# Split weights interleaved, every second GEMM group run backward, other places for rows and weights, and no widened products, in a two-layer decoder trunk

## The chip, the core and the metric

The kernel runs on one core of a Trainium2 chip. The time is the device time of one execution in microseconds. Two runs of the kernel before took 2280.04 and 2280.48 us, median 2280.26 us. The profile comes from one execution with the hardware profiler on.

The engines are named as in the profile: PE is TensorE (matrix products), PEld its loads of stationary operands, DVE is VectorE, ACT is ScalarE, POOL is GpSimd, SP is SyncE, which here only issues DMAs.

## The reference

The input is 256 rows of 2048 features with 16 meta tokens in front (272 rows in all), and two layers follow. Layer 0 is a forgetting attention, layer 1 a stick-breaking attention whose keys and values come from one shared projection. Each layer ends in a squared-ReLU MLP of width 8192. Cut to its matrix products:

```python
a = rms_norm(h, norm_attn[0]); q, k, v, f = split(a @ fox_w_in[0])     # 2048 -> 3*2048 + 16
h = h + forgetting_attention(q, k, v, cumsum(log_sigmoid(f + b))) @ fox_w_o[0]
h = h + square(relu(rms_norm(h, norm_mlp[0]) @ w_up[0])) @ w_down[0]   # 2048 -> 8192 -> 2048
a = rms_norm(h, norm_attn[1]); k, v = split(rms_norm(h, kv_norm) @ w_kv)
h = h + stick_breaking_attention(a @ sb_w_q[0], k, v) @ sb_w_o[0]
h = h + square(relu(rms_norm(h, norm_mlp[1]) @ w_up[1])) @ w_down[1]
return rms_norm(h, final_norm)[16:]
```

Everything is float32. After the keys and values of layer 1, the 16 meta rows are needed no more.

## The kernel before

**Split operands.** Activations are kept with features on the 128 partitions, as 16 chunks of 128 features by T = 272 rows. A GEMM is made from split operands: each float32 is written as a high part (a copy to `fp32r`) and a low part (the difference), and a product is three products: high by high, low rows by high weights, high rows by low weights.

**Groups.** All GEMMs go through `gemm_group`. One group takes 2048 input features and 512 output features. It holds four PSUM accumulators (`accs[m]`, 128 output features each) and loops over four blocks `kb` of 512 input features, each of four chunks `kc`. That makes 4 x 4 x 4 x 3 = 192 products; the stationary operand of each is a 128x128 piece of split weights, and the moving operand is one chunk of split rows: 272 columns in layer 0 and in the shared keys and values (t0 = 0), 256 columns where the meta rows are left out (t0 = 16, `M`). The variable `u` counts the groups from 1 to 96. The last one, u = 96, is `token_group`: there the rows are stationary and the 512 weight columns move.

The order of stages is: 12 groups for queries, keys and values of layer 0 with the attention among them; 4 for its output projection; 32 for its MLP (for each of four quarters `f` of the width 4 up and 4 down); 4 for the queries of layer 1; 8 for the shared keys and values; 4 for the output projection; 31 plus the token group for the MLP of layer 1.

**Weights.** `weights` loads one block of weights for one `kb` with two DMAs on SP's queue into two tiles `raw` (2 chunks by 512 columns each), four buffers deep, and splits them: ACT copies to the high part (L225), DVE subtracts for the low part (L226). The high and the low parts are in tiles of their own (`whi`, `wlo`, [128, 2, 576], four buffers each), and 512 of the 576 columns are used from `o1` on: 0 at t0 = 0, 16 at t0 = 16.

**Rows.** `Split` holds split rows: 16 chunks with a stride of XROW = 640 elements, the high part at element `hi` of a chunk's stretch, the low part at `lo`. `ROWS` gives these places: (48, 368) at t0 = 0 and (0, 320) at t0 = 16.

**Widened products.** At t0 = 16, `Split` fills six columns behind the 256 of the high rows with zeros (on POOL, L135). In every group with u % 4 == 1 there, and in the group u = 90, three products on the high rows run over 262 columns rather than 256 (`wide`). What they add behind column 256 of the accumulator is not read.

**Order on the engines.** A scheduler places the instructions. Products are kept in the order of the program; other matrix products (attention scores, transposes, norms) come between them. The evacuation of an accumulator belongs to the end of its group: `evac` reads `accs[m][:, :n]` on DVE, and the output of the up stage is squared and split again into the rows `u` (`Split(f"u{layer}_{f}", t0)`).

Of the kernel before, what the change touches and what calls it, by code (L numbers as in the profile page):

```python
# [10 lines left out]
F32R = mybir.dt.float32r  # L11
# [4 lines left out]
P = 128  # L16
D = 2048
NC = D // P
# [6 lines left out]
N_FF = 4  # L25

ROWS = {0: (48, 368), M: (0, 320)}
XROW = 640

G_A0, G_M0, G_KV, G_A1, G_M1, G_FIN = range(6)  # L30
# [3 lines left out]
def yoco_kernel(ctx: ExitStack, tc: tile.TileContext, hT_in, gains, b_f, w_f, w_qkv0, w_o0, w_up, w_dn,  # L34
                w_kv, w_q1, w_o1, g_row, out):
    nc = tc.nc
# [5 lines left out]
    wspl = ctx.enter_context(tc.tile_pool(name="wspl", bufs=4))  # L42
# [72 lines left out]
    pad = align.tile([P, 32], F32, name="pad")  # L115
# [5 lines left out]
    class Split:  # L121


        def __init__(self, label, t0):
            n = T - t0
            self.t0 = t0
            rows = xs.tile([P, NC * XROW + 64], F32R, tag="x", name=f"x_{label}")
            hi, lo = ROWS[t0]
            rows = rows[:, hi:hi + NC * XROW].rearrange("p (c t) -> p c t", c=NC)
            d = lo - hi  # L130
            self.hi, self.lo = rows[:, :, :n], rows[:, :, d:d + n]
            if t0:

                self.wide = rows[:, :, :n + 6]
                nc.gpsimd.tensor_copy(rows[:, :, n:n + 6], pad[:, :6].unsqueeze(1).to_broadcast([P, NC, 6]))  # L135

    def split_chunk(sp, gi, c):

# [47 lines left out]
    def behind(ins, other):  # L186
        tc.add_manual_dep(ins.ins, other.name, mybir.DependencyInfo(mybir.DependencyClass.NoSync,
                                                                    mybir.DependencyReason.DATA))

    def gemm_matmul(*args, **kw):  # L190

        ins = nc.tensor.matmul(*args, **kw).ins  # L192
# [8 lines left out]
    def weights(u, kb, wblk, o1, load_x=None):  # L201

        src_w = wblk[kb].rearrange("p (k c) -> p k c", k=4)
        piece = 1 if load_x is not None and kb < 2 else 2
        raws = [wraw.tile([P, 2, 512], F32, tag="raw", name=f"raw_{u}_{kb}_{hf}") for hf in range(2)]
        for k0 in range(0, 4, piece):
            if load_x is not None:
                load_x(range(4 * kb + k0, 4 * kb + k0 + piece))
            if load_x is not None and kb == k0 == 0:

                for c0 in (0, 256):
                    nc.scalar.dma_start(raws[0][:, 0, c0:c0 + 256], src_w[:, 0, c0:c0 + 256])
            else:
                nc.sync.dma_start(raws[k0 // 2][:, k0 % 2:k0 % 2 + piece], src_w[:, k0:k0 + piece])
        parts = []
        for hf in range(2):
            whi, wlo = (wspl.tile([P, 2, 576], F32R, tag=f"w{x}", name=f"w{x}_{u}_{kb}_{hf}") for x in ("hi", "lo"))
            whi, wlo = whi[:, :, o1:o1 + 512], wlo[:, :, o1:o1 + 512]
            boxes = [(o, piece, 0, 512) for o in range(0, 2, piece)]
            if load_x is not None and kb == hf == 0:  # L220
                boxes[:1] = [(0, 1, 0, 256), (0, 1, 256, 512)]
            for o, no, c0, c1 in boxes:
                src = raws[hf][:, o:o + no, c0:c1]
                hp, lp = whi[:, o:o + no, c0:c1], wlo[:, o:o + no, c0:c1]
                on_act = nc.scalar.activation(hp, src, AF.Copy)  # L225
                on_dve = nc.vector.tensor_tensor(out=lp, in0=src, in1=hp.bitcast(F32), op=ALU.subtract)  # L226
            parts.append((whi, wlo))
        return parts, on_act, on_dve

    def gemm_group(wblk, sp, t0, evac, before={}, after={}, load_x=None):  # L230

        uid[0] += 1
        u = uid[0]
        accs = [pacc.tile([P, 512], F32, tag="acc", name=f"acc_{u}_{m}") for m in range(4)]
        n = T - t0
        for kb in range(4):
            if kb in before:
                before[kb]()  # L240
            parts, on_act, on_dve = weights(u, kb, wblk, 16 if t0 else 0, load_x)
            if kb in after:
                with tc.issue_after(on_act.ins), tc.issue_after(on_dve.ins):
                    after[kb]()

            if load_x is not None and kb == 0:
                runs = [([kc], range(4)) for kc in range(4)]
            elif kb in (0, 3):
                runs = [(range(4), [m]) for m in range(4)]
            else:  # L250
                runs = [(range(2 * hf, 2 * hf + 2), range(4)) for hf in range(2)]
            pinned[0] = load_x is None
            for kcs, ms in runs:
                pairs = ((0, sp.hi), (0, sp.lo), (1, sp.hi))
                if t0:
                    products = [(kc, m, *pair) for pair in pairs for kc in kcs for m in ms]
                else:
                    products = [(kc, m, *pair) for m in ms for kc in kcs for pair in pairs]
                left = {m: 3 * len(kcs) for m in ms}

                wide = [(0, 0, 0), (1, 0, 1), (2, 1, 1)] if t0 and u % 4 == 1 else []
                if u == 90:

                    wide = [(0, 0, 0), (0, 0, 1), (0, 2, 1)]
                for kc, m, part, x in products:
                    first, left[m] = kb == kc == 0 and left[m] == 3 * len(kcs), left[m] - 1
                    nw = n
                    if m == (0 if u == 90 else 3) and x is sp.hi and (kb, kc, part) in wide:
                        x, nw = sp.wide, n + 6
                    gemm_matmul(accs[m][:, :nw], parts[kc // 2][part][:, kc % 2, m * P:(m + 1) * P], x[:, 4 * kb + kc],  # L270
                                start=first, stop=kb == kc == 3 and left[m] == 0)
                if kb == 3:
                    for m in ms:
                        evac(m, accs[m][:, :n])

    def token_group(wblk, sp, done):


        uid[0] += 1
        u = uid[0]  # L280
# [12 lines left out]

        for kb in range(2):
            parts.append(weights(u, kb, wblk, 16)[0])
            for b in range(2):
                products(b, [kb])
        for kb in (2, 3):
            parts.append(weights(u, kb, wblk, 16)[0])
# [324 lines left out]
    def mlp(layer, xm, norm, t0, last_evac, last_group=None):  # L624
# [5 lines left out]
        for f in range(N_FF):  # L630
            u = Split(f"u{layer}_{f}", t0)
            for g in range(4):
                def evac(m, acc, g=g):
                    c = 4 * g + m
                    r = tmp.tile([P, T], F32, tag="relu", name=f"relu_{layer}_{f}_{c}")
                    u2 = tmp.tile([P, T], F32, tag="u2", name=f"u2_{layer}_{f}_{c}")
                    nc.vector.scalar_tensor_tensor(out=r[:, t0:], in0=acc, scalar=0.0, in1=box["r"][:, t0:],
                                                   op0=ALU.max, op1=ALU.mult)
                    nc.scalar.activation(u2[:, t0:], r[:, t0:], AF.Square)
                    nc.scalar.activation(u.hi[:, c], u2[:, t0:], AF.Copy)  # L640
                    nc.vector.tensor_tensor(out=u.lo[:, c], in0=u2[:, t0:], in1=u.hi[:, c].bitcast(F32),
                                            op=ALU.subtract)
                gemm_group(w_up[layer, f, g], xm, t0, evac, {2: get_rstd} if f == g == 0 else {})
                if last_group is not None and f == N_FF - 1 and g == 0:
                    to_token_major()
            for g in range(4):
# [304 lines left out]
```

## Time and profile before

| what | value |
|---|---|
| median time, two runs | 2280.26 us |
| span of the profiled execution | 2278.5 us |
| time around the span, against the median | 1.8 us |
| HBM read, written | 413.85 MB, 8.41 MB |
| mean DMA rate | 187 GB/s |
| DVE busy | 1333.5 us |
| ACT busy | 1065.1 us |

The span is the time from the first to the last instruction of the profiled execution. A row of a group of instructions gives line, engine, operation, output and inputs by the program's names, shapes and count, then busy time and the mean duration of one, then the idle time of the engine ahead of it and what ended it. The mean duration of a product is from its issue to its modelled end; products overlap, so the next one starts well before that. The view of the chain of waits in order of time gives the start, the length and what ran; "x192" behind it is the number of instructions in the run, so length by number is the distance from one start to the next.

The weights come in by these issues (line 6 of the page: destination and source, queue, count, size, time to landing), and none of them stands in the chain outside the first microseconds:

```profile
raw<-w_up SPq DMA_DIRECT2D x256, 512.0 KB, 3.9
raw<-w_dn SPq DMA_DIRECT2D x256, 512.0 KB, 4.0
```

### The profile page before, as it was taken

The numbers are of one execution on the slowest core, as the hardware profiler recorded it, in microseconds if no ns is written. First come the engines' busy times: TensorE is split into PE (matmuls) and PEld (weight loads), VectorE is DVE, ScalarE is ACT, GpSimd is POOL, SyncE is SP. The second block draws the span as 40 slices with busy tenths as digits, with TensorE's granted clock in tenths as the row PEclk, the third lists the DMA queues.
The fourth block names the chain that finished last, engine by engine and source line by source line (L and its number), as shares of the span: only waits on it lengthen the run. The fifth ranks groups of instructions, "written<-read, shape, count | busy, mean of one in ns | idle before, by whom it ended". The sixth has DMA issues, their size and how long they took to land.

```text
span 2278.5 us, 44956 instructions
## 1 busy us (share of the span) xinstructions
PE 2271.1 (100%) x18898; PEld 2262.8 (99%) x18898; DVE 1333.5 (59%) x1930; ACT 1065.1 (47%) x1471; POOL 39.4 (2%) x72
## 2 busy tenths in 40 slices
PE   9999999999999999999999999999999999999998
PEld 9999999999999999999999999999999999999998
DVE  7767566554455455455566666666555555555555
ACT  6444445443354344335445555555443544543554
POOL 1000000000000000000000000000000000000001
PEclk9999999999999999999999999999999999999999
DMA  7765665555555555555556555555656556566564
GB/s 238 228 198 188 222 184 176 181 172 180 182 176 185 167 185 179 174 185 169 186 183 193 168 174 169 167 185 190 202 187 201 192 189 201 184 200 195 186 201 141
DMA packets 146171, 425.19 MB, mean 187 GB/s; under 512 B 31648, under 2 KB 43824, under 8 KB 145968
## 3 DMA queue, kind: packets, MB, share of 16 engines
q1 hardware_dynamic: 113760, 406.29, 54.1%
q10 hardware_dynamic: 32208, 16.02, 2.6%
q8 instruction: 148, 2.42, 0.4%
q14 instruction: 55, 0.45, 0.1%
HBM read 413.85 MB, written 8.41 MB: 185 GB/s over the span
## 4 chain that ended last, share of the span: by engine, by line
PE 99%; DMA 0%; issue 0%; POOL 0%; SPq 0%; POOLq 0%; ACT 0%; DVE 0%
PE acc L192 97%; PE po L435 0%; PE ps L435 0%; PE pza L435 0%; DMA raw<-w_qkv 0%; PE pzb L735 0%; PE po L804 0%; PE ps L508 0%; PE po L603 0%; PE pf L354 0%; PE pta L757 0%; PE pta L756 0%; PE pv L394 0%; POOL ob L850 0%; PE ptb L709 0%
## 5 line engine op out<-in xcount | busy, mean ns | idle before, releaser
L226 DVE TENSOR_TENSOR wlo<-raw,whi 128x1024 fp32r<-128x1024 f32 (+1 forms) x773 | 928.5, 1216 | 715.6 <-ACT whi L225 706.6
L225 ACT ACTIVATE whi<-raw 128x1024 fp32r<-128x1024 f32 (+1 forms) x773 | 796.4, 1050 | 961.0 <-PE acc L192 913.4
L192 PE MATMUL acc<-x_m,whi 128*128 128x272 f32 (+1 forms) x4096 | 643.1, 282 | 0.0
L192 PE MATMUL acc<-x_u,whi 128*128 128x272 f32 (+1 forms) x3968 | 626.0, 282 | 0.0
L192 PEld LDWEIGHTS acc<-x_m,whi 128*128 128x128 f32 x4096 | 566.0, 188 | 0.1
L192 PEld LDWEIGHTS acc<-x_u,whi 128*128 128x128 f32 x3968 | 550.4, 188 | 0.0
L192 PE MATMUL acc<-x_m,wlo 128*128 128x272 f32 (+1 forms) x2048 | 441.4, 282 | 0.0
L192 PE MATMUL acc<-x_u,wlo 128*128 128x272 f32 (+1 forms) x1984 | 432.1, 282 | 0.0
L192 PE MATMUL acc<-x_a,whi 128*128 128x272 f32 (+1 forms) x2048 | 355.4, 286 | 0.2 <-ACT whi L225 0.2
L192 PEld LDWEIGHTS acc<-x_m,wlo 128*128 128x128 f32 x2048 | 323.5, 188 | 0.0
L192 PEld LDWEIGHTS acc<-x_u,wlo 128*128 128x128 f32 x1984 | 315.3, 188 | 0.0
L192 PEld LDWEIGHTS acc<-x_a,whi 128*128 128x128 f32 x2048 | 301.3, 189 | 1.7 <-ACT whi L225 1.1
L192 PE MATMUL acc<-x_a,wlo 128*128 128x272 f32 (+1 forms) x1024 | 253.8, 286 | 0.0
L192 PE MATMUL acc<-x_kv,whi 128*128 128x272 f32 x1024 | 191.7, 288 | 0.0
L192 PEld LDWEIGHTS acc<-x_a,wlo 128*128 128x128 f32 x1024 | 175.7, 188 | 0.7 <-DVE ssq_a L158 0.4
L192 PE MATMUL acc<-x_o,whi 128*128 128x272 f32 (+1 forms) x1024 | 163.1, 283 | 0.0
L192 PEld LDWEIGHTS acc<-x_kv,whi 128*128 128x128 f32 x1024 | 160.1, 189 | 0.1
L192 PE MATMUL acc<-x_kv,wlo 128*128 128x272 f32 x512 | 147.6, 288 | 0.0
L192 PEld LDWEIGHTS acc<-x_o,whi 128*128 128x128 f32 x1024 | 142.3, 188 | 0.0
L307 DVE TENSOR_TENSOR hT<-acc,hT 128x272 f32<-128x272 f32 (+1 forms) x156 | 67.3, 431 | 75.4 <-PE acc L192 75.2
L192 PE MATMUL acc<-x_o,wlo 128*128 128x272 f32 (+1 forms) x512 | 110.7, 282 | 0.0
L192 PEld LDWEIGHTS acc<-x_kv,wlo 128*128 128x128 f32 x512 | 96.6, 189 | 0.0
(255 smaller groups left out, 1065.5 us busy)
## 6 DMA issues: line engine op xcount, KB each, us to landing
raw<-w_up SPq DMA_DIRECT2D x256, 512.0 KB, 3.9
raw<-w_dn SPq DMA_DIRECT2D x256, 512.0 KB, 4.0
raw<-w_qkv SPq DMA_DIRECT2D x92, 512.0 KB, 4.3
raw<-w_o SPq DMA_DIRECT2D x64, 512.0 KB, 3.9
raw<-w_kv SPq DMA_DIRECT2D x64, 512.0 KB, 4.4
raw<-w_q SPq DMA_DIRECT2D x32, 512.0 KB, 4.7
p_dram<-raw_p ACTq DMA_DIRECT2D x32, 96.0 KB, 4.6
v_dram<-turned ACTq DMA_DIRECT2D x48, 64.0 KB, 3.8
```

The costliest lines, as they stand in the source:

```text
L192: ins = nc.tensor.matmul(*args, **kw).ins
L225: on_act = nc.scalar.activation(hp, src, AF.Copy)
L226: on_dve = nc.vector.tensor_tensor(out=lp, in0=src, in1=hp.bitcast(F32), op=ALU.subtract)
L307: nc.vector.tensor_tensor(out=hT[:, c, t0:], in0=acc, in1=hT[:, c, t0:], op=ALU.add)
```

## The change

Four things are changed in the GEMMs. The number of products, their order, the DMAs and the evacuations are as before.

1. High and low weights lie in one tile `w` ([128, 2, 1152]), alternating: column c's high part at element 2c, its low part at 2c + 1. A stationary operand is now read with a step of two elements, and ACT's and DVE's splits write with that step. `token_group` keeps the two parts apart in the tile (`apart=True`), contiguous as before.
2. In groups with odd `u`, `turn` reverses the moving rows and the accumulator: the same columns, from the last to the first.
3. Places. The u rows of the MLPs stand at `ROWS_OF`: high at 16f + 8, low at 16f + 328, in both layers. The weights of the up groups start at column 8f of the interleaved tile (`shift`), that is at element 16f; all other weights start at 0 at both t0. Rows other than u stay where they were.
4. The widened products and the fill behind the rows are gone.

```diff
+ROWS_OF = {f"u{layer}_{f}": (16 * f + 8, 16 * f + 328) for layer in range(2) for f in range(N_FF)}
...
-            hi, lo = ROWS[t0]
+            hi, lo = ROWS_OF.get(label, ROWS[t0])
...
-            if t0:
-
-                self.wide = rows[:, :, :n + 6]
-                nc.gpsimd.tensor_copy(rows[:, :, n:n + 6], pad[:, :6].unsqueeze(1).to_broadcast([P, NC, 6]))
...
+    def backward(a):
+
+        *outer, (step, n) = a.ap
+        return bass.AP(a.tensor, a.offset + (n - 1) * step, [*outer, (-step, n)])
...
-            whi, wlo = (wspl.tile([P, 2, 576], F32R, tag=f"w{x}", name=f"w{x}_{u}_{kb}_{hf}") for x in ("hi", "lo"))
-            whi, wlo = whi[:, :, o1:o1 + 512], wlo[:, :, o1:o1 + 512]
+            both = wspl.tile([P, 2, 1152], F32R, tag="w", name=f"w_{u}_{kb}_{hf}")
+            if apart:
+                whi, wlo = (both[:, :, o:o + 512] for o in (0, 576))
+            else:
+                pairs = both[:, :, 2 * o1:2 * o1 + 1024].rearrange("p k (c x) -> p k c x", x=2)
+                whi, wlo = pairs[:, :, :, 0], pairs[:, :, :, 1]
...
+        turn = backward if u % 2 else lambda a: a
...
-            parts, on_act, on_dve = weights(u, kb, wblk, 16 if t0 else 0, load_x)
+            parts, on_act, on_dve = weights(u, kb, wblk, shift, load_x)
...
-                wide = [(0, 0, 0), (1, 0, 1), (2, 1, 1)] if t0 and u % 4 == 1 else []
-                if u == 90:
-
-                    wide = [(0, 0, 0), (0, 0, 1), (0, 2, 1)]
...
-                    nw = n
-                    if m == (0 if u == 90 else 3) and x is sp.hi and (kb, kc, part) in wide:
-                        x, nw = sp.wide, n + 6
-                    gemm_matmul(accs[m][:, :nw], parts[kc // 2][part][:, kc % 2, m * P:(m + 1) * P], x[:, 4 * kb + kc],
+                    gemm_matmul(turn(accs[m][:, :n]), parts[kc // 2][part][:, kc % 2, m * P:(m + 1) * P], turn(x[:, 4 * kb + kc]),
...
-            parts.append(weights(u, kb, wblk, 16)[0])
+            parts.append(weights(u, kb, wblk, 0, apart=True)[0])
...
-                gemm_group(w_up[layer, f, g], xm, t0, evac, {2: get_rstd} if f == g == 0 else {})
+                gemm_group(w_up[layer, f, g], xm, t0, evac, {2: get_rstd} if f == g == 0 else {}, shift=8 * f)
```

More of the change, by code (lines that the diff above doesn't have):

```diff
@@ L199, in gemm_matmul, with weights @@
         issued.append(ins)
-    def weights(u, kb, wblk, o1, load_x=None):
+    def weights(u, kb, wblk, o1, load_x=None, apart=False):
         src_w = wblk[kb].rearrange("p (k c) -> p k c", k=4)
@@ L228, in weights, with gemm_group @@
         return parts, on_act, on_dve
-    def gemm_group(wblk, sp, t0, evac, before={}, after={}, load_x=None):
+    def gemm_group(wblk, sp, t0, evac, before={}, after={}, load_x=None, shift=0):
         uid[0] += 1
@@ L298, in token_group @@
         for kb in (2, 3):
-            parts.append(weights(u, kb, wblk, 16)[0])
+            parts.append(weights(u, kb, wblk, 0, apart=True)[0])
         later = None
```

## The prediction, made before the changed kernel was run

> **What bounds the kernel now.** I read the page first (busy shares, then the clock row), then the chain of waits in order of time, because on a kernel whose TensorE is never idle only the pace of its products is left to change.
>
> ```profile
> span 2278.5 us, 44956 instructions
> ...
> PE 2271.1 (100%) x18898; PEld 2262.8 (99%) x18898; DVE 1333.5 (59%) x1930; ACT 1065.1 (47%) x1471; POOL 39.4 (2%) x72
> ...
> PEclk9999999999999999999999999999999999999999
> ...
> PE 99%; DMA 0%; issue 0%; POOL 0%; SPq 0%; POOLq 0%; ACT 0%; DVE 0%
> ```
>
> TensorE is busy for 2271.1 of 2278.5 us, its granted clock is at the top in every slice, and the chain is 99% PE. Nothing waits for a transfer or for VectorE, so the time is a number of products times the start-to-start pace of a product. The mean of a row (282 ns) is not that pace, because products overlap. The chain in order of time gives it: start, length and count of unbroken runs of products.
>
> ```profile
> 69.41 12.16 PE acc L192 x96
> ...
> 111.81 23.69 PE acc L192 x192
> ...
> 439.65 733.95 PE acc L192 x5951
> ```
>
> These are 272-column products (layer 0). Two runs give 23.69/192 = 123.4 ns and 733.95/5951 = 123.3 ns, but the first gives 12.16/96 = 126.7 ns, for the same kind of product on the same tiles. The 256-column products of layer 1:
>
> ```profile
> 1184.76 0.46 PE pms_a L163 x2
> 1185.22 2.59 PE acc L192 x22
> ...
> 1188.17 71.86 PE acc L192 x634
> ...
> 1493.92 87.43 PE acc L192 x770
> 1581.35 0.43 PE pms_m L163 x2
> ...
> 1599.92 490.15 PE acc L192 x4324
> ...
> 2115.15 0.87 PE ph L826 x8
> ```
>
> Here 490.15/4324 = 113.4 ns and 71.86/634 = 113.3 ns, but 2.59/22 = 117.7 ns just after the fp32 products of a norm at 1184.8 us. So a product has two paces, a good one and a slow one: 123.3 and 126.7 ns at 272 columns (3.4 ns apart), 113.4 and 117.7 ns at 256 columns (4.3 ns apart). The slow one starts after a disturbance and lasts; it ends between the two runs at 1185 and 1188 us, and the groups of the window from 1187.77 to 1187.87 us hold the third widened product of that group:
>
> ```profile
> L192 PE MATMUL acc<-x_a,wlo 128*128 128x262 f32 x1 | 0.3, 284 | 0.0
> ```
>
> The changed parts (place of rows and weights, direction, widened products) all touch what sets this pace, and none changes how many products there are.
>
> **The change part by part.** Counts first.
>
> ```profile
> L192 PE MATMUL acc<-x_m,whi 128*128 128x272 f32 x2048 | 379.3, 287 | 0.0
> ...
> L192 PE MATMUL acc<-x_u,wlo 128*128 128x272 f32 x1024 | 293.9, 287 | 0.0
> ...
> L192 PE MATMUL acc<-x_m,whi 128*128 128x256 f32 x2043 | 263.2, 277 | 0.0
> ...
> L192 PE MATMUL acc<-x_m,wlo 128*128 128x262 f32 x10 | 2.7, 279 | 0.0
> ```
>
> A group issues 4 x 4 x 4 x 3 = 192 products. At 272 columns there are 56 groups, 10752 products (32 MLP groups of layer 0 are 6144 of them: 2048 + 1024 on x_m and as many on x_u, the rows shown). At 256 columns there are 39 groups, 7488 products (33 of them widened to 262). The token group adds 96 products of 512 columns; it keeps contiguous weights (`apart`) and I give it nothing.
>
> *Widened products go.* Thirty-three products lose 6 of 262 columns: at the good pace of 113.4/256 = 0.44 ns per column that is 33 x 2.7 ns = 0.1 us. The seven fills of the pad columns go too:
>
> ```profile
> L135 POOL CAST x_u<-pad 128x96 fp32r<-128x96 f32 x4 | 1.1, 267 | 612.1 <-PE acc L192 612.1
> ```
>
> They take 0.3 us each on POOL, which is 2% busy, hidden behind the products of the stage before; worth nothing. What counts is what the widened products end. Four stretches of layer 1 follow a disturbance (the rows at 1184.8, 1493.9, 1581.4 and 2115.2 us): 1185 to the key and value stage at 1261, 1494 to 1581, 1582 to 2115 and 2116 to the last group at 2252 us, 832 us together. If each stayed slow to its end, 832 x (117.7/113.4 - 1) = 32 us; if the next group (21.8 us) ended it, 4 x 21.8 x 0.038 = 3 us. So 3 to 32 us.
>
> *Weights interleaved.* Each weight load now steps over 8 bytes per column and spans twice the bytes. The loader's own speed stands in these rows:
>
> ```profile
> L192 PEld LDWEIGHTS acc<-x_u,whi 128*128 128x128 f32 x3968 | 550.4, 188 | 0.0
> ...
> L354 PEld LDWEIGHTS pf<-hT,wf 128*32 128x32 f32 x32 | 0.8, 109 | 0.7
> ...
> L362 PEld LDWEIGHTS pf_sum<-parts,both 128*16 128x16 f32 x2 | 0.1, 94 | 0.1
> ```
>
> From 32 to 128 columns the duration grows by 79 ns, 0.82 ns per column, so 128 columns stream for about 105 ns and 83 ns is fixed. A load runs under the product before it, so it has 113.4 - 105 = 8 ns of cover at 256 columns and 123.3 - 105 = 18 ns at 272. The products at the very end show what a load leaves free:
>
> ```profile
> 2269.18 2.62 PE L192 MATMUL idle_fin<-mean_w 128*128 128x128 f32 x22
> ```
>
> They have 128 columns and still follow each other at (2.62 - 0.28)/21 = 111 ns: the 105 ns and some 6 to hand over. No row here shows a strided load. From below: a load that hides as before costs 0. From above: one that takes twice as long (210 + 6) sets a pace of 216 ns on every product. I take a value near the low end, because the loader is slow (one column in 0.82 ns against 0.44 to 0.45 ns for the moving side) and so has time to fetch more bytes: it adds lines to fetch beside the moving rows, hence the slow pace, but does not become the bound. The Trainium skill (SBUF — State Buffer, Specifications (TRN2)) states lines of 16 bytes and full bandwidth from two hits per line; a step of 8 bytes makes exactly two, so by it the load costs nothing, and no run here shows it yet.
>
> The splits on ACT and DVE write, and DVE also reads, with the same step.
>
> ```profile
> L226 DVE TENSOR_TENSOR wlo<-raw,whi 128x1024 fp32r<-128x1024 f32 (+1 forms) x773 | 928.5, 1216 | 715.6 <-ACT whi L225 706.6
> L225 ACT ACTIVATE whi<-raw 128x1024 fp32r<-128x1024 f32 (+1 forms) x773 | 796.4, 1050 | 961.0 <-PE acc L192 913.4
> ```
>
> At 1.19 ns (DVE) and 1.03 ns (ACT) per column they are as slow as one element at a time; I take no change. Their cover is idle time: DVE has 2278.5 - 1333.5 = 945 us. If the step doubled L226 (+928 us), DVE would be as busy as TensorE, and only then would the stream stall.
>
> *Places.* Layer 0's rows outside the MLP's u stay at 48 and 368 with weights at 0, as before. Layer 1's weights move from 16 to 0 (up groups: 0, 16, 32, 48 elements in the interleaved tile), and the u rows of both layers from 48 or 0 to 8, 24, 40, 56. Bounded by the two paces: 0 to 3.4 ns per product at 272, 0 to 4.3 ns at 256; below nothing, by one such step less, since the trace shows no pace under 123.3 and 113.3 in a long run but also no other place.
>
> *Odd groups backward.* 48 groups read rows and write PSUM with step -1. No row shows it. The nearest rows are again the two paces; above them lies a stream served at part rate, priced with the rivals. I take the two paces. The start of each group also changes phase against the group before, which can start a slow stretch as well as end one.
>
> *Queues.* Loads on SP, splits, evacuations and their order stay; no wait is added.
>
> **The sum.** I take the slow pace where both the weights' layout and the place change: all of layer 1 and the MLP of layer 0. Layer 1: 7488 x 4.3 ns = 32 us (the lost widened products are in this, not beside it). Layer 0's MLP: 6144 x 3.4 ns = 21 us. The other 4608 products at 272 columns keep rows at 48 and their 18 ns of cover: 0. Together 53 us on the span of 2278.5: 2331.5. The median of 2280.3 stands 1.8 us above the span, so 2333 us, 2.3% slower.
>
> **The rivals.**
>
> *Not slower: only the cure is lost.* Interleaving, places and direction are hidden, as the 8 and 18 ns of cover allow, and only the widened products' 3 to 32 us come: 2283 to 2312 us, about 2292. For it: layer 0 has no widened products and still runs 734 us at 123.3 ns. Against it: the first run above shows slow stretches in layer 0 too, with the old place. It decides if the good pace still appears in most groups. The Trainium skill (SBUF — State Buffer, Who interferes with whom) gives PE two independent read ports and says that it never waits on anyone, which would leave places without effect; the two paces on one kind of product do not fit that.
>
> *Faster.* Before, a load passes 512 bytes in 105 ns while the rows pass 1024 in 113 ns, so the two reads overtake; interleaved, the load passes 1024 in 105 ns and the two march side by side. If the pace is set by where these reads meet, a fixed distance could remove one step (3.4 ns), as ending a slow stretch does: 18240 x 3.4 = 62 us less, 2218 us; on forward groups alone, half, 2249 us. It decides where a group's pace falls under 120 or 110 ns. Against it: eight places are used at once, and not all can be the best.
>
> *Much slower: a part-rate stream.* Once load and hand-over pass 113 ns they are the pace. At 20% longer (126 + 6 = 132 ns): 7488 x 18.6 + 10752 x 8.7 = 233 us, 2513 us; at twice, 216 ns: 7488 x 102.6 + 10752 x 92.7 = 1765 us, 4045 us. The same holds for backward rows. The Trainium skill (PSUM — Partial Sum Buffer, Specifications (TRN2)) gives lines of 8 bytes and says that a non-contiguous pattern slows matmuls significantly; whether a step of -1 counts as one it does not say.
>
> **How the numbers follow.** Forecast (slow pace in layer 1 and layer 0's MLP) 0.42; only the cure lost 0.27; faster 0.15; part rate 0.16. The predicted time is the forecast's 2333 us. About 2%, 46 us, is what a measurement of this kernel can tell from no change: slower is the forecast and part rate, 0.58; within 2% is the lost cure, 0.27; faster 0.15. The range goes down to 2249 us (faster on forward groups alone; some 0.08 is below) and up to 2470, where a load about 10 to 20% too long ends (some 0.11 above). The forecast's own range is 2312 (layer 1 alone) to 2349 us (all 10752 products of 272 columns slow).
>
> **What would show it.** Right: unbroken runs at 117 to 118 ns in layer 1 and near 126.7 ns in layer 0's MLP, TensorE still at 100%, DVE and ACT shares as now. The lost cure: 113.4 ns in most groups, slow runs only after norms. Faster: runs under 120 or 110 ns. Part rate: runs above 130 ns, all groups (load) or every second group (direction); or the mean of L226 and L225 up and TensorE with idle time. If odd and even groups or the four f differ strongly, the sum over both was the wrong form, even if the total comes out.

## The result, and the profile after

The changed kernel takes 2354.73 us (median of two runs, 2354.23 and 2355.24 us) against 2280.26 us: 1.0326 times as long, with a 95% interval of 1.0296 to 1.0356. It is 3.3% slower. The forecast was 2333 us, with 2312 to 2349 us as its own range, so the measured time lies somewhat above that range.

The page of the changed kernel, the same parts as of before (busy time, granted clock, chain, then two groups of splits and two of weight loads):

```profile
span 2352.5 us, 44927 instructions
...
PE 2344.7 (100%) x18898; PEld 2336.4 (99%) x18898; DVE 1337.1 (57%) x1930; ACT 1143.6 (49%) x1471; POOL 35.4 (2%) x65
...
PEclk9999999999999999999999999999999999999999
...
PE 99%; DMA 0%; issue 0%; POOL 0%; SPq 0%; POOLq 0%; ACT 0%; DVE 0%
...
L232 DVE TENSOR_TENSOR w<-raw,w 128x1024 fp32r<-128x1024 f32 (+1 forms) x773 | 931.2, 1219 | 814.4 <-ACT w L231 812.0
L231 ACT ACTIVATE w<-raw 128x1024 fp32r<-128x1024 f32 (+1 forms) x773 | 883.6, 1165 | 962.3 <-PE acc L194 901.0
...
L194 PEld LDWEIGHTS acc<-x_m,w 128*128 128x128 f32 x6144 | 752.0, 195 | 0.1
...
L194 PEld LDWEIGHTS acc<-w,x_u 128*128 128x128 f32 x96 | 17.8, 188 | 4.1
```

Nothing new waits: the number of products is the same (18898), the clock is at the top in every slice, the chain is 99% TensorE. The rows of the loads with the step of two elements say 195 ns instead of 188; the token group, whose operands stayed contiguous, still has 188. ACT's split went from 1050 to 1165 ns, in idle time.

So the 74 us are in the pace of the products. The chain of waits in order of time, asked for stretches that lie within one group each (start, length, what, count; the length over the count is the pace):

```profile
449.18 24.32 PE acc L194 x192
...
522.14 23.77 PE acc L194 x191
...
738.15 24.32 PE acc L194 x192
...
1148.12 24.83 PE acc L194 x191
...
1771.16 23.05 PE acc L194 x192
...
1794.21 22.50 PE acc L194 x191
...
1816.83 22.92 PE acc L194 x191
```

These are, in order: 126.7 ns (layer 0, first up groups), 124.5 ns (a backward group of the first down stage), 126.7 ns (a forward group), 130.0 ns (a group of the last down stage), then in layer 1 120.1 ns (down stage of f = 0), 117.8 ns (backward, f = 1) and 120.0 ns (forward, f = 1). No 256-column group is left at 113.3 ns and no 272-column group at 123.3 ns. From the start of each stage's first product to the start of the next stage's, in both traces:

| stage | products | pace before, ns | pace after, ns | cost, us | forecast, us |
|---|---|---|---|---|---|
| layer 0: queries, keys, values, output projection | 3072 | 123.8 | 126.8 | 9.0 | 0 |
| layer 0: MLP | 6144 | 123.3 | 125.8 | 15.1 | 21 |
| shared keys and values | 1536 | 123.4 | 126.9 | 5.3 | 0 |
| layer 1: queries, output projection, MLP f = 0 | 3072 | 113.5 | 120.0 | 19.9 | 13 |
| layer 1: rest of the MLP | 4416 | 113.4 | 118.9 | 24.4 | 19 |
| sum | 18240 | | | 73.7 | 53 |

The spans differ by 2352.5 - 2278.5 = 74.0 us, so next to nothing else is left to explain.

### The profile page after: what moved, and what is told of

It reads as the page before. It is cut to its first block, busy times and chain, and to the rows that moved or that the text cites. A ratio compares the mean times of both kernels' runs of the same rounds, so it can differ in the third digit from the quotient of the medians.

```text
span 2352.5 us, 44927 instructions
## 1 busy us (share of the span) xinstructions
PE 2344.7 (100%) x18898; PEld 2336.4 (99%) x18898; DVE 1337.1 (57%) x1930; ACT 1143.6 (49%) x1471; POOL 35.4 (2%) x65
## 4 chain that ended last, share of the span: by engine, by line
PE 99%; DMA 0%; issue 0%; POOL 0%; SPq 0%; POOLq 0%; ACT 0%; DVE 0%
PE acc L194 97%; PE po L435 0%; PE ps L435 0%; PE pza L435 0%; DMA raw<-w_qkv 0%; PE pzb L735 0%; PE po L804 0%; PE ps L508 0%; PE po L603 0%; PE pf L354 0%; PE pta L757 0%; PE pta L756 0%; PE pv L394 0%; POOL ob L850 0%; PE ptb L709 0%
## 5 line engine op out<-in xcount | busy, mean ns | idle before, releaser
L232 DVE TENSOR_TENSOR w<-raw,w 128x1024 fp32r<-128x1024 f32 (+1 forms) x773 | 931.2, 1219 | 814.4 <-ACT w L231 812.0
L231 ACT ACTIVATE w<-raw 128x1024 fp32r<-128x1024 f32 (+1 forms) x773 | 883.6, 1165 | 962.3 <-PE acc L194 901.0
L194 PE MATMUL acc<-x_m,w 128*128 128x272 f32 (+1 forms) x6144 | 753.3, 285 | 0.0
L194 PEld LDWEIGHTS acc<-x_m,w 128*128 128x128 f32 x6144 | 752.0, 195 | 0.1
L194 PE MATMUL acc<-x_u,w 128*128 128x272 f32 (+1 forms) x5952 | 732.5, 286 | 0.0
L194 PEld LDWEIGHTS acc<-x_u,w 128*128 128x128 f32 x5952 | 731.7, 195 | 0.0
L194 PE MATMUL acc<-x_a,w 128*128 128x272 f32 (+1 forms) x3072 | 396.8, 289 | 0.7 <-ACT w L231 0.7
L194 PEld LDWEIGHTS acc<-x_a,w 128*128 128x128 f32 x3072 | 388.6, 196 | 2.4 <-issue 1.3
L194 PE MATMUL acc<-x_kv,w 128*128 128x272 f32 x1536 | 199.7, 291 | 0.0
L194 PEld LDWEIGHTS acc<-x_kv,w 128*128 128x128 f32 x1536 | 196.5, 196 | 0.1
```

## The experiments

Two theories stood at the start. *Load*: the interleaved weight load is longer, and that sets the slower pace. *Phase*: direction, places and the lost widened products decide where the two reads of TensorE (moving rows, weights) stand against each other. After the first four runs I put the second in a wider form, *meet*: the reads get in each other's way at a pace that step, direction and place together decide, so that the parts do not add. The runs of whole kernels, in the order of their sections (the two runs with added products stand in the section on the load by itself):

| run | what | median, us | ratio to before | 95% interval |
|---|---|---|---|---|
| e1_interleave | before, interleaved | 2372.08 | 1.0400 | 1.0384 to 1.0415 |
| e2_backward | before, odd groups backward | 2307.72 | 1.0116 | 1.0100 to 1.0133 |
| e3_no_wide | before, no widened products | 2286.49 | 1.0026 | 1.0017 to 1.0036 |
| e4_places | before, new places | 2329.93 | 1.0215 | 1.0199 to 1.0230 |
| f1_no_interleave | changed, contiguous weights | 2335.10 | 1.0237 | 1.0222 to 1.0252 |
| f2_forward | changed, all forward | 2366.64 | 1.0377 | 1.0359 to 1.0394 |
| f3_all_backward | changed, all backward | 2344.26 | 1.0279 | 1.0262 to 1.0297 |
| f4_old_places | changed, old places | 2355.63 | 1.0326 | 1.0311 to 1.0342 |
| s1_scan | 16 places, contiguous | 2328.47 | one run | |
| s2_scan_interleaved | 32 places, interleaved | 2361.41 | one run | |

### One part of the change alone

**Interleaving.** Old places, all forward, widened products kept; `token_group` contiguous.

```diff
-            whi, wlo = (wspl.tile([P, 2, 576], F32R, tag=f"w{x}", name=f"w{x}_{u}_{kb}_{hf}") for x in ("hi", "lo"))
-            whi, wlo = whi[:, :, o1:o1 + 512], wlo[:, :, o1:o1 + 512]
+            both = wspl.tile([P, 2, 1152], F32R, tag="w", name=f"w_{u}_{kb}_{hf}")
...
+                pairs = both[:, :, o1:o1 + 1024].rearrange("p k (c x) -> p k c x", x=2)
+                whi, wlo = pairs[:, :, :, 0], pairs[:, :, :, 1]
```

> The kernel before with the split weights interleaved, and nothing else: old places, all groups forward, widened products kept. Theory 'load' (the strided weight load is longer and sets or disturbs the pace of every product): nearly all of the 74.5 us comes with this part, 2335 to 2355 us, 256-column runs at 118 to 120 ns, 272-column runs above 125 ns, load rows near 195 ns. Theory 'phase' (the slow pace comes from direction, places and the missing cure): 2280 to 2288 us, runs at 113.4 and 123.3 ns.

Measured: +91.8 us, more than the whole change and more than either theory gave. Chain of waits, a group of layer 0's MLP and one of layer 1's queries:

```profile
474.73 24.41 PE acc L192 x191
...
1257.29 22.80 PE acc L192 x190
```

127.8 and 120.0 ns, in all groups of their kinds but the MLP's first, which a norm divides; the other 272-column groups stand at 126.7 to 127.6. With these paces the sum closes: 7488 x 6.7 + 6144 x 4.5 + 4608 x 3.3 ns = 50 + 28 + 15 = 93 us. Its load rows say 195 to 196 ns and ACT's split 1149 ns as in the changed kernel, so these two belong to the interleaving. What follows: the interleaving alone is enough for a slow pace everywhere, and takes it further than the 117.7 ns that the trace of before knew.

**Odd groups backward.**

```diff
+        turn = backward if u % 2 else lambda a: a
...
-                    gemm_matmul(accs[m][:, :nw], parts[kc // 2][part][:, kc % 2, m * P:(m + 1) * P], x[:, 4 * kb + kc],
+                    gemm_matmul(turn(accs[m][:, :nw]), parts[kc // 2][part][:, kc % 2, m * P:(m + 1) * P], turn(x[:, 4 * kb + kc]),
```

> The kernel before with odd groups backward, and nothing else; contiguous weights. Theory 'load': 2278 to 2285 us, odd and even groups at the same pace. Theory 'phase': odd groups at the slow pace or at a pace of their own, 2300 to 2320 us.

Measured: +27.4 us. A backward and a forward 256-column group, one after the other:

```profile
1760.72 22.50 PE acc L197 x191
...
1783.33 21.78 PE acc L197 x192
...
705.10 23.75 PE acc L197 x190
```

117.8 and 113.4 ns; the last row is a backward group of 272 columns, 125.0 ns. The loads stay at 188 ns. So a reversed read with a reversed write to PSUM costs 4.4 or 1.7 ns per product here, which is nothing near a part-rate stream. A longer load is not seen in this run and so does not explain its slow pace.

**No widened products.**

```diff
-                wide = [(0, 0, 0), (1, 0, 1), (2, 1, 1)] if t0 and u % 4 == 1 else []
+                wide = []
```

> The kernel before without its 33 widened products. Either theory: the slow pace of 117.7 ns is no longer ended after a disturbance in layer 1. If it then lasts to the next disturbance, 2312 us; if the next group ends it, 2283 us. Theory 'load' says that this cost isn't in the changed kernel, where all paces are others.

Measured: +6.2 us. Two 256-column groups, in the queries and in the MLP of layer 1:

```profile
1218.99 22.02 PE acc L192 x187
...
1598.79 21.53 PE acc L192 x190
```

Once other products have brought the slow 117.8 ns on in the first group of the queries, it stays to their end, and the same happens in the output projection. It then lasts into layer 1's MLP, up to the norm inside the first group:

```profile
1575.92 11.54 PE acc L192 x98
1587.46 0.43 PE pms_m L163 x2
1587.89 12.14 PE acc L192 x107
```

The products run at 117.8 ns ahead of the norm's two products and at 113.5 ns behind them, and the rest of the MLP has 113.3 ns. In the kernel before the same norm came at 1581.35 us behind a good stretch and began a slow one. So such a disturbance can end a slow stretch as well as begin one. The queries, the output projection and the MLP's first up stage are 2.9, 2.9 and 0.3 us longer than before, which is nearly the whole loss. The widened products do end a slow stretch in the first two, but the loss is near the low end of 3 to 32 us.

**Places.** Contiguous weights, forward, widened kept; weights start at 16f elements in the up groups and at 0 elsewhere, u rows at 16f + 8.

```diff
-            hi, lo = ROWS[t0]
+            hi, lo = ROWS_OF.get(label, ROWS[t0])
...
-            parts, on_act, on_dve = weights(u, kb, wblk, 16 if t0 else 0, load_x)
+            parts, on_act, on_dve = weights(u, kb, wblk, shift, load_x)
```

> The kernel before with the new places alone: u rows at 8, 24, 40, 56 and their low parts 320 behind, weights of the up groups at 0, 16, 32, 48 elements of their contiguous tiles, other weights at 0; widened products kept. Theory 'load': under 10 us, 2280 to 2290 us. Theory 'phase': slow paces (117.7 and 126.7 ns) in those stages whose place is bad, 2300 to 2335 us.

Measured: +49.6 us. A group of layer 1's queries (rows at 0, weights at 0) and one of the up stage f = 1 (rows at 0, weights at 16, the old distance):

```profile
1232.30 22.80 PE acc L193 x190
...
1796.74 21.76 PE acc L193 x192
```

120.0 against 113.3 ns, with the same instructions, contiguous loads, direction and widened products. So the place alone moves the pace, and it reaches the 120.0 ns of interleaving with contiguous loads. *Load* as the only cause falls. The place of the rows counts too: with the weights at 0, the down groups of layer 1 run at 117.8, 120.0, 118.7 and 118.3 ns with rows at 8, 24, 40 and 56. The first of these:

```profile
1707.58 22.38 PE acc L193 x190
```

The sum of the four single parts is 92 + 27 + 6 + 50 = 175 us, against 74 for all together: the parts do not add.

### The changed kernel with one part undone or carried further

**Contiguous weights at the same places.**

```diff
-                whi, wlo = (both[:, :, o:o + 512] for o in (0, 576))
+                whi, wlo = (both[:, :, o + 2 * o1:o + 2 * o1 + 512] for o in (0, 576))
...
-            parts, on_act, on_dve = weights(u, kb, wblk, shift, load_x)
+            parts, on_act, on_dve = weights(u, kb, wblk, shift, load_x, apart=True)
```

> The changed kernel with contiguous weights at the same start bytes; direction, places and missing widened products as changed. Theory 'load' (the step makes a weight load longer, and that is what the changed kernel pays): most of the loss goes, under 2325 us, load rows 188 ns. Theory 'meet' (the reads of moving rows and of weights get in each other's way, and step, direction and place each only move where they do): the single parts' costs of 27, 50 and 6 us stay, 2340 to 2365 us, although no load is longer.

Measured: 2335.10 us, 19.6 us less than the changed kernel, not 92 less. The time lies between the two expectations, under 2325 and 2340 to 2365 us, and confirms neither. Chain of waits, a forward group at f = 0 and two at f = 1 of layer 1 (u = 74 and 76), and the loads:

```profile
1617.99 22.91 PE acc L194 x191
...
1799.43 22.61 PE acc L194 x192
...
1844.65 21.55 PE acc L194 x190
```

```profile
L194 PEld LDWEIGHTS acc<-x_u,w 128*128 128x128 f32 x5952 | 726.6, 188 | 0.0
```

119.9, 117.8 and 113.4 ns, with loads of 188 ns on average. The last two are a riddle: same place (rows 0, weights 16), same direction, same step, no widened products, and yet two paces. The run of the places alone had 113.3 to 113.4 ns in all four of these groups. So two paces are possible at one place, as the queries without widened products showed; what chooses between them was not tried.

**All groups forward, and all backward.**

```diff
-        turn = backward if u % 2 else lambda a: a
+        turn = lambda a: a
```

> The changed kernel with all groups forward. Parts add: it gives back what backward alone cost on the kernel before, 27 us, so 2327 us. 'Meet' (off the good place direction costs nothing more, and backward even helped): odd groups run as the even ones did, 120.0 ns in layer 1 and about 126.7 in layer 0's MLP, so the 2.2 ns on the odd groups from layer 1's f = 1 on and about 1.5 ns on some twelve of layer 0 are lost again: 2360 to 2372 us.

In the other run the line is `turn = backward`.

> The changed kernel with all groups backward. Theory 'meet': even groups of the MLPs go from 120.0 to 117.8 ns (layer 1, from the second quarter on, 12 groups) and from 125.9 or 126.7 to 124.4 ns (layer 0, some 10 groups), 5 + 4 us less: about 2346 us. Theory 'load': nothing, 2352 to 2357 us.

Measured: 2366.64 and 2344.26 us, 11.9 us more and 10.5 us less than the changed kernel. The same group of layer 1 (f = 1, u = 74) first forward, then backward:

```profile
1822.83 23.04 PE acc L194 x192
```

```profile
1811.61 22.50 PE acc L194 x191
```

120.0 and 117.8 ns. On the kernel before, backward cost 27 us; under interleaved weights it gains 11 us for each half of the groups. The sign of one part depends on the others, which *meet* expected and an adding of parts (2327 us for all forward) rules out. Backward does not help every interleaved group: in the changed kernel's layer 1, queries, output projection and f = 0 have 120.0 ns in both directions. And a forward group is not always like itself: u = 82 runs at 121.1 ns here and at 120.0 ns in the changed kernel, where backward groups stand around it.

**Old places.**

```diff
-            hi, lo = ROWS_OF.get(label, ROWS[t0])
+            hi, lo = ROWS[t0]
...
-            parts, on_act, on_dve = weights(u, kb, wblk, shift, load_x)
+            parts, on_act, on_dve = weights(u, kb, wblk, 8 if t0 else 0, load_x)
```

> The changed kernel with all rows and all weights at their old places (rows 48 and 368 or 0 and 320; weights from element 0 or 16), still interleaved, odd groups backward, no widened products. Parts add: it gives back the 50 us that the places alone cost, so 2305 us. 'Meet' (the old place is good only for contiguous forward reads): even groups as with interleaving alone, 120.0 and 126.7 to 127.8 ns, odd groups about 2.2 ns under that, so some 2350 us, no better than the changed kernel by more than 5 us.

Measured: 2355.63 us, the time of the changed kernel, where an adding of parts gives 2305. A backward and a forward group of layer 1, and a forward one of layer 0's MLP:

```profile
1796.80 22.50 PE acc L194 x191
...
1819.42 22.92 PE acc L194 x191
...
741.79 24.32 PE acc L194 x192
```

117.8, 120.0 and 126.7 ns in every group of these kinds; the backward groups of layer 0's MLP have 126.6 ns, so no gain there, where 2.2 ns was expected. Once the weights are interleaved, the old places are in all worth nothing over the new ones, but that is a sum of two parts: layer 0's MLP is 5.3 us longer at the old places, and layer 1 is 3.8 us shorter.

### Is there a place where it is free?

Both scans keep rows at 48 (layer 0) or 0 (layer 1), run forward, have no widened products, and give each of the 16 pairs (f, g) of the MLP another start of the weights.

```diff
-                gemm_group(w_up[layer, f, g], xm, t0, evac, {2: get_rstd} if f == g == 0 else {})
+                gemm_group(w_up[layer, f, g], xm, t0, evac, {2: get_rstd} if f == g == 0 else {}, o1=16 * f + 4 * g)
...
-                    gemm_group(w_dn[layer, f, g], u, t0, evac)
+                    gemm_group(w_dn[layer, f, g], u, t0, evac, o1=16 * f + 4 * g)
```

**Contiguous.**

> The kernel before, forward, contiguous weights, no widened products, with the weights of MLP group (f, g) at element 16f + 4g: 16 places from 0 to 60 against rows at 0 (layer 1) and 48 (layer 0), each in an up and a down group. Theory 'meet': the pace follows the distance of weights from rows; 113.4 ns at element 16 and its neighbours in layer 1, 123.3 ns at element 0 in layer 0 and near it, and 117 to 120 or 125 to 127 ns at most others; 2300 to 2340 us. Theory 'load': one pace at all places, 2284 to 2290 us.

Measured: 2328.47 us. Paces (ns) by the element at which the weights start, from the trace; up and down groups agree to about 0.2 ns, but for the start 36 at 256 columns, where the up group has 118.3 and the down group 119.9 ns:

| start | 0 | 4 | 8 | 12 | 16 | 20 | 24 | 28 | 32 | 36 | 40 | 44 | 48 | 52 | 56 | 60 |
|---|---|---|---|---|---|---|---|---|---|---|---|---|---|---|---|---|
| 272 columns | 123.3 | 126.7 | 123.4 | 126.7 | 126.7 | 123.4 | 126.7 | 126.7 | 126.7 | 125.7 | 125.8 | 125.0 | 125.4 | 125.0 | 126.6 | 126.7 |
| 256 columns | 120.0 | 118.3 | 118.3 | 117.8 | 113.3 | 118.8 | 117.3 | 120.0 | 118.7 | 118.3 | 120.0 | 118.1 | 117.8 | 116.7 | 116.7 | 120.0 |

The chain of the group that starts at 16 in layer 1:

```profile
1772.88 21.53 PE acc L192 x190
```

At 256 columns one place of 16 gives 113.3 ns, the one that the kernel before used; at 272 columns three of 16 give 123.3 to 123.4, the old start 0 among them. No place beats these. *Load*, one pace at all places, fails. *Meet* holds in the total and in the spread, but the neighbours of the good places are not good (starts 12 and 20 have 117.8 and 118.8 ns, start 4 has 126.7), and the distance of weights from rows is not all that counts: of the eight down stages of the run with the places alone, four have the pace that the scan shows at the same distance modulo 64 elements, and four miss it by 1.1 to 1.4 ns.

**Interleaved**, starts at 32f + 8g (up) and 32f + 8g + 4 (down).

> The kernel before with interleaved weights, all forward, no widened products, rows at their old places; the weights of the MLP group (f, g) start at element 32f + 8g in the up groups and at 32f + 8g + 4 in the down groups, 32 places in all. 'Load' (the strided load is too long wherever it starts): 120.0 ns in all groups of layer 1 and 127.8 in those of layer 0's MLP, whatever the place; in all about 2372 us. 'Meet' (the step shifts where the reads meet): paces between 113.3 and 120.0 and between 123.3 and 128 by place, as without interleaving, and some place is within 1 ns of 113.3 or of 123.3; in all 2330 to 2365 us.

Measured: 2361.41 us. Places matter here too: 118.3 to 122.2 ns at 256 columns, 124.5 to 128.3 at 272 (leaving out the very first MLP group, which a norm divides), and a start 64 elements on has the same pace to 0.1 ns at 272 columns, and at 256 columns in all but three pairs in the last two stages (off by 0.5 to 1.7 ns), so it counts modulo 256 bytes. *Load*, with 120.0 and 127.8 ns at every place, falls here as well; but the half of the other expectation fails that some place would come within 1 ns of 113.3 or 123.3. The best groups:

```profile
474.38 23.77 PE acc L192 x191
...
1704.79 22.55 PE acc L192 x190
```

124.5 and 118.7 ns (another group has 118.3). With rows at these places and forward reads, interleaving costs at least 1.1 ns at 272 columns and 5.0 ns at 256 at every start tried. No version was found that beats the kernel before.

### The load by itself

Sets of equal products were added behind the end of the kernel before (its output is not touched): moving columns, step of the weight columns and start of the weights vary. The first run had 32 products a set:

```diff
+    for n in (64, 256):
+        for step in (1, 2, 4, 8):
+            pb = pacc.tile([P, 512], F32, tag="acc", name=f"bench_{n}_{step}")
+            for i in range(32):
+                gemm_matmul(pb[:, :n], bench[:, 2048:2048 + 128 * step].rearrange("p (c x) -> p c x", x=step)[:, :, 0],
+                            bench[:, 0:n], start=True, stop=True)
```

> The kernel before with 256 products added behind the end (and two copies that fill their operands): 32 each with 64 and with 256 moving columns, weights with a step of 1, 2, 4 and 8 elements. With 64 columns the load alone sets the pace. Theory 'load': 111 ns at step 1 and 118 ns or more at step 2. Theory 'meet': 111 ns at steps 1 and 2 with 64 columns, 118 to 120 ns at step 2 only with 256 columns. Either: more at steps 4 and 8, if a longer way between columns costs at all.

It told little, because the granted clock was 0.51 for the first 28 us (window from 2275 to 2303 us): 64 columns took 213.3 ns at steps 1 and 2. At the full clock, which came back at the end of the fifth set, 256 columns gave 120.0 ns at step 2, 233.3 at step 4 and 241.2 at step 8. The second run put 384 products of 256 columns ahead, had 64 a set, and varied start and direction too:

```diff
+    sets = [(256, 1, 0, 0)] * 6 + [(64, 1, 0, 0), (64, 2, 0, 0), (64, 4, 0, 0), (128, 1, 0, 0), (128, 2, 0, 0),
+                                   (256, 1, 0, 0), (256, 1, 16, 0), (256, 1, 16, 1), (256, 2, 0, 0), (256, 2, 0, 1),
...
+    for k, (n, step, o, back) in enumerate(sets):
```

> The kernel before, with 22 sets of 64 products added behind its end, all on the same moving rows (they start at element 0 of their tile). The first six sets only bring the clock back; the rest vary the moving columns (64, 128, 256), the step of the 128 weight columns (1, 2, 4 elements), the element at which they start (0, 16, 32, 48) and, in two sets, the direction. 'Load': a load with step 2 is itself longer at full clock; with 64 and with 128 moving columns, where the load alone sets the pace (about 111 ns), step 2 is 6 to 12 ns slower than step 1, and the rows of the loads are as much longer. 'Meet': with 64 and 128 columns step 1 and step 2 have the same pace to 1 ns; at 256 columns step 1 runs at 120.0 ns from element 0 and at 113.3 ns from element 16, and step 2 at 117 to 120 ns at every start. For both, step 4 takes over 200 ns.

Chain of waits, one set each: 256 columns at step 1 from 0, step 1 from 16, step 2 from 0; then 128 columns at step 2; then 64 and 256 columns at step 4:

```profile
2284.57 7.56 PE bench L192 x63
...
2399.40 7.42 PE bench L192 x63
...
2414.48 7.56 PE bench L192 x63
...
2375.87 13.65 PE bench L192 x64
...
2347.46 14.21 PE bench L192 x61
...
2452.88 14.82 PE bench L192 x64
```

That is 120.0, 117.8, 120.0, 213.3, 233 and 232 ns. The windows of the same trace (stretch, its length, busy time of PE and the other engines, then the granted clock) say which clock held, for the last three sets and for a set of 64 columns ahead of them:

```profile
2323.00:2325.00 2.00, 2.00 (x21) 2.00 (x20) 0.00 (x0) 0.00 (x0) 0.00 (x0) 1.00 0.00 0
...
2348.00:2361.00 13.00, 13.00 (x57) 13.00 (x58) 0.00 (x0) 0.00 (x0) 0.00 (x0) 0.50 0.00 0
...
2377.00:2389.00 12.00, 12.00 (x58) 12.00 (x57) 0.00 (x0) 0.00 (x0) 0.00 (x0) 0.50 0.01 1
...
2454.00:2467.00 13.00, 13.00 (x57) 13.00 (x57) 0.00 (x0) 0.00 (x0) 0.00 (x0) 1.00 0.00 0
```

The decisive comparison failed: the short products lost the full clock (0.50) before step 2 came, so whether a strided load alone is longer at the full clock stays open. At half clock 128 columns take 213.3 ns at step 1 and at step 2, so there it costs nothing. Step 4 takes 233.3 ns from start to start at either clock (mean of each set's records), so the granted clock does not set that pace; I read it as the fetch of the weights, which is argued and not shown. If the fetch goes by the bytes passed over, step 2 needs half, 117 ns: an estimate from that row. It can hold up to step 4 at most, since step 8 takes 241.2 ns and not twice 233. Such a fetch would be hidden under half-clock products and would not be under 113.3 ns ones, and no interleaved 256-column group of any run is under 117.8 ns; but it would hide under 123.3 ns, where the interleaved kernels still run at 124.4 to 130.0. So a longer fetch can be a part of the cost at 256 columns, and not the whole. The other expectation held for step 2 (120.0 to 120.1 ns at the four starts and backward) and missed for the start at 16 with step 1: 117.8 ns there, not 113.3.

## Why the prediction was right, and where it was not

**The bound was read rightly.** Only the pace could change, and only it did: TensorE 100%, clock full, chain 99% TensorE, 73.7 of 74.0 us in the runs of products. Reading length over count from the chain, not the mean of a row, made this visible.

**Products take a slow pace: right in kind, mis-sized in three terms.** The slow paces were taken from disturbed stretches of the kernel before, 117.7 and 126.7 ns.
- *Layer 1, 7488 x 4.3 ns = 32 us*: 44.3 us. The interleaved forward pace is 120.0 ns, 6.7 above the good one and not in the trace of before; only the backward groups from f = 1 on have the 117.8 ns that was forecast for all.
- *Layer 0's MLP, 6144 x 3.4 ns = 21 us*: 15.1 us. Here the backward groups of twelve odd positions run at 124.5 ns, which the trace of before did not show either, some forward ones too, while the last down stage is above the slow pace, at 128 to 130 ns.
- *The other 4608 products: 0 us, because rows stay at 48 and a load has 18 ns of cover*: 14.3 us. This step failed. The interleaving run alone, at the old places, has 126.7 to 127.6 ns there, so cover in this sense does not protect: load plus hand-over, set against the length of the moving stream, does not give the pace.

Two terms that are short by 12 and 14 us and one that is long by 6 make the 21 us between 53 and 74. Taking one slow pace for several causes together, rather than adding their costs, was the sound part of the sum: the parts alone add up to 175 us. But that the total came as near as it did owes something to luck. Interleaving alone costs 92 us, and the forecast gave the other parts no gain; interleaving with backward groups and without widened products, still at the old places, takes 2355.63 us against 2372.08.

**The widened products' loss, 3 to 32 us**, measured 6.2 us alone. It was rightly put inside layer 1's term; in the changed kernel the good pace never comes back, so there is nothing for them to restore unless they heal interleaved groups too, which was not tried. The interleaving run kept them and ran at 120.0 ns throughout, which speaks against it. That a slow stretch starts after a disturbance and lasts was half of what the traces show: without the widened products, layer 1's MLP norm ended one.

**Places and direction, bounded by the two paces.** Alone they cost 50 and 27 us, inside the bounds at 272 columns and, with 120.0 ns, outside them at 256. The gain that the bound of the places allowed, a pace under 113.3 or 123.3 ns, never came; the 2.2 ns that backward saves in some interleaved groups is saved from a slower pace.

**"The load does not become the bound"** is half settled: the loads' rows grew by 7 ns to 195, step 2 costs no load time at half clock, and contiguous loads show the same 120.0 ns. A part of the 7 ns goes with the pace and not with the step: at 120.0 ns the rows of contiguous loads say 189 ns (scan, start 28) to 192 (places alone, queries). Whether a longer load has a share in the cost at 256 columns remains open. The Trainium skill (SBUF — State Buffer, Specifications (TRN2)) asks for two hits in a 16-byte line for full bandwidth, which a step of 8 bytes makes; the interleaving run, 120.0 against 113.3 ns with nothing else changed, shows that this rule does not make the step free here.

**ACT's and DVE's splits, no change**: DVE 1216 to 1219 ns, right; ACT 1050 to 1165 ns, wrong by 11%, and hidden as the idle time allowed.

**The rivals.** *Only the cure lost* asked for 113.4 ns in most groups: none. *Faster, the reads march side by side*: no group came under 113.3 or 123.3 ns in any run. Its idea that the meeting of two reads sets the pace contradicts no run, but none shows it; its sign was wrong. *Part rate*: no group over 130.0 ns, TensorE without idle time; at the full clock only steps of four and eight elements reach it. *Two independent read ports* (the Trainium skill, SBUF — State Buffer, Who interferes with whom): by it TensorE never waits on anyone, which would leave places without effect. The contiguous scan, 113.3 to 120.0 ns by the start of the weights alone, contradicts that, whatever the mechanism.

**The form of the sum.** The prediction named as a sign against itself that odd and even groups or the four f differ strongly. They do: 117.8 against 120.0, 124.5 against 126.7, f = 0 unlike f = 1. A product of count and one slow pace per width was the wrong form even though the time came out near. What the experiments put in its place is a pace that step, direction and place set together, and what ran just before as well, since one combination can show two paces. The kernel before sits at the best combination found. Any one part leaves it, and the others then add little or take some back: interleaving +92, places +50, backward +27, no widened products +6 alone; undone in the changed kernel, interleaving gives back 19.6 us and places nothing (+0.9 us), and all groups forward costs 11.9 more.

Whether reads collide, which ones, and by what rule, was argued and not shown: there is no record of a single read in the trace. What chooses between the two paces of one combination is open as well.

## What to carry to other kernels

Where TensorE is never idle, read the pace as length over count in the chain of waits, group by group, and treat a tuned placement as one point of a joint setting: measure each part alone and undone, because single costs (175 us) and the joint cost (74 us) need not be near each other. Don't take the slowest pace in the trace of before as the ceiling for a layout that the trace does not contain, and don't give a stage zero for cover that no row has tested. Before giving weights a step, scan the start of the contiguous ones; here the starts differ by up to 6.7 ns of a 113 ns product. One group per start is not enough for that, since one start can show two paces.

## What was not expected of the hardware

- The start of the stationary operand shifts the pace of equal products by up to 6.7 ns at 256 columns and 3.4 ns at 272 (contiguous scan). With interleaved weights nearly all starts 64 elements (256 bytes) apart agree to 0.1 ns.
- One place can hold two paces: at start 16 with rows at 0, forward and contiguous, 113.3 ns in the scan, and 117.8 and 113.4 ns in two groups of the changed kernel with contiguous weights.
- Two fp32 products of a norm between equal products can move the pace from 113.3 to 117.8 ns and, in another run, from 117.8 to 113.3 ns.
- A reversed moving read together with a reversed PSUM write costs 1.7 to 4.4 ns on the kernel before, and saves about 2.2 ns in some groups with interleaved weights and nothing in others.
- Weights at a step of four elements give 233 ns from product to product at half clock (against 213 at steps one and two) and at full clock (against 120 at step two); a step of eight adds only 8 ns at full clock.
- Products of 64 columns, back to back with TensorE shown as fully busy, let the granted clock fall from 1.00 to 0.50 some 3 us after they began, while 256-column products at 233 ns from start to start kept 1.00 for the 15 us that they ran.
